# A hybrid encoder trunk on one core: gating values in the buffers of squares, the row of norms ahead in ScalarE's queue, first weights by single contraction steps

## The chip, the core and the metric

The kernel runs on one core of a Trainium2 chip. The core has TensorE (PE in the profile; its weight loads, which overlap, are PEld), VectorE (DVE), ScalarE (ACT), GpSimd (POOL) and SyncE (SP), which here only issues DMAs. TensorE reads its operands from on-chip memory and writes its sums into PSUM, of which this kernel uses eight banks of 128 x 512 floats. The metric is the device time in microseconds (us); lower is better.

## The reference

One layer over x (2048 x 1024, float32). The rows of x are normed by their root mean square, and one projection of 1024 x 2816 gives eleven slots of 256 columns, which four mixers share:

```python
h = rmsnorm(x, norm_g); proj = h @ w_in
a_u, a_v, a_g, b_q, b_k, b_v, b_g, c_in, c_g, d_q, d_g = split(proj, 11)
y_a = a_u * spatial_gating(layernorm(a_v)) * silu(a_g)       # 128x128 mixing per chunk and head
y_b = neighbourhood_attention(b_q, b_k, b_v) * silu(b_g)     # 8x16 windows on a 32x64 grid, 4 heads
y_c = fourier_mixing(c_in) * silu(c_g)                       # real part of a 2-D DFT, linear map
y_d = memory_attention(d_q, mem) * silu(d_g)                 # 256 memory tokens, 4 heads
out = x + concat(y_a, y_b, y_c, y_d) @ w_out
```

Queries and keys of both attentions are normed per head of 64.

## The kernel before

**Precision.** Nearly every product is made of three: each operand is split into a rounded part (hi) and the rest (lo), and hi x hi, hi x lo and lo x hi are summed in PSUM. The split of x is an ACTIVATE on ScalarE with the norm's weights as scale (L137) and a DVE instruction for lo (L138); the split of weights is a cast on ScalarE (L217, L229) and a subtraction on POOL or DVE (L219, L231).

**Order.** TensorE's instructions stand in the order in which the program writes them. A driver keeps a modelled time t, runs tasks that are due (attention, transposes, the Fourier part) and fills in products of projections otherwise; a task says by `yield d` after how many modelled us it wants to go on. The order of all other engines, SP's loads among them, is planned when the program is built: of what is ready in a planned run the instruction with the lowest number goes first, and `hp(n)` lowers the number by n. Each engine then works its list strictly in order. Buffers and banks are given out in the planned order as well; a tile waits until the buffer's former user is done.

**Stages.** The rows are worked in halves of 1024 (h = 0, 1). The first projection does two slots side by side, c_in with its accumulators in the four banks "acc", and d_q (`alt`) in the banks "sc" and "mi" (two each); it goes through the eight contraction steps k of 128 rows one by one. In each step come four groups, each of three products of c_in with 512 columns and six of d_q with 256. `get_w` loads weights for two steps at once (128 x 2 x 256, 256 KB) into one of five buffers "raw" and splits them. Eighteen transposes of a constant go ahead of the first product. `stats` squares the rows of x on ScalarE (L291) and gives rstd. `do_dq` norms d_q per head (`head_norm`: squares into one of two buffers "sq", L376; sums, L378) and transposes it in four parts. `bcast` transposes rstd into a bank "mi", copies it on ScalarE into a row (L302), writes it out and reads it back on all partitions. `mem_kv` projects the memory tokens and norms the keys, using "sq" too (L505, L376).

`pair_vv` then projects a_v and b_v together, in two passes u of 96 products of 512 columns, with four accumulators that hold 256 columns of each. `evac_vv` frees them: for each of four row tiles ScalarE or DVE scales the gating values a_v into half of a tile `va` (L456, L454), ScalarE writes hi of b_v (L459), DVE lo (L460), and SP stores b_v to V (L463). `va` (two per pass) and the tiles of b_v (four) all come from the five buffers "nat". `do_a` norms the gating values and TensorE reads them in `s_mix`, with 4.0 and 1.5 modelled us between. Then come a_u, the pair b_q and b_k, the gates and the same for the second half; d_0's attention, the Fourier part and the neighbourhood attention run beside them as tasks, the attentions through `pipeline`, which runs scores two units ahead of transposes. The output projection ends the program.

## Time and profile before

| | us |
|---|---|
| time of the kernel, median of 3 runs | 872.89 (871.86 to 875.16) |
| the profiled execution, its own time | 873.72 |
| its span in the profile | 872.0 |
| PE busy | 852.2 (98%), 4448 instructions |
| DVE busy | 501.8 (58%) |
| ACT busy | 407.4 (47%) |
| POOL busy | 327.3 (38%) |
| DMA | 177.88 MB, mean 204 GB/s |

Times in the profile count from the start of the span. Matmuls are pipelined, and the end of one is modelled, so busy shares of PE say where it stood still rather than how well it worked. "PEclk" is the clock that was granted to TensorE, as a share of full speed; it has two levels, 2.4 and 1.2 GHz (1.00 and 0.50). A bracket behind an instruction is the idle time of its engine before it, and what ended that.

### The profile page before, as it was taken

How to read it: one execution, taken by the hardware profiler on the slowest of the kernel's cores; microseconds unless marked ns; L12 is line 12 of the kernel's file. 1: busy time of each engine (PE TensorE's matmuls, PEld its weight loads, DVE VectorE, ACT ScalarE, POOL GpSimd, SP SyncE). 2: the span in 40 equal slices, each digit the busy share in tenths (PEclk: the TensorE clock that was granted, in tenths of full speed). 3: DMA queues.
4: the chain of work that ended last, by engine and by line, in shares of the span. 5: the costliest groups of instructions: out<-in, count | busy, mean ns of one | idle time of the engine just before them, and what ended most of it. 6: DMA issues, size and time to landing. Idle time of an engine off the chain costs nothing.

```text
span 872.0 us, 13653 instructions
## 1 busy us (share of the span) xinstructions
PE 852.2 (98%) x4448; PEld 713.5 (82%) x4448; DVE 501.8 (58%) x1064; ACT 407.4 (47%) x930; POOL 327.3 (38%) x368
## 2 busy tenths in 40 slices
PE   8999899999999999999999999999998999999998
PEld 7987688888788878887789888888877888888886
DVE  5355565587532557765454876676798778741111
ACT  5674353466742543544324644666767445521110
POOL 1136331154332122552232723434557333235550
PEclk9999999999999999999999999999999999999999
DMA  8957643346762562469759797864598986556661
GB/s 268 332 197 226 194 137 103 119 117 179 230 186 98 191 218 85 135 169 272 221 180 320 248 306 250 260 215 145 171 307 247 343 258 219 173 167 198 190 215 72
DMA packets 147463, 177.88 MB, mean 204 GB/s; under 512 B 29232, under 2 KB 105152, under 8 KB 147392
## 3 DMA queue, kind: packets, MB, share of 16 engines
q1 hardware_dynamic: 145104, 170.33, 62.4%
q0 software_dynamic: 1728, 6.29, 2.4%
q8 instruction: 35, 0.57, 0.3%
q10 hardware_dynamic: 560, 0.40, 0.1%
q14 instruction: 36, 0.29, 0.1%
HBM read 132.92 MB, written 44.05 MB: 203 GB/s over the span
## 4 chain that ended last, share of the span: by engine, by line
PE 72%; DMA 12%; DVE 6%; ACT 4%; issue 3%; POOL 2%; SPq 0%; ACTq 0%; DVEq 0%; POOLq 0%
PE acc L147 55%; PE w L147 8%; PE w L151 4%; PE sc L147 3%; PE mi L147 2%; DMA G<-st 2%; DMA nat<-in_mem 1%; DMA QD<-st 1%; DMA raw<-in_xT 1%; DVE PT L535 1%; POOL hss L125 1%; DMA kk<-KB 1%; DMA nat<-O 1%; DMA qq<-QB 1%; ACT P L918 1%
## 5 line engine op out<-in xcount | busy, mean ns | idle before, releaser
L147 PE MATMUL acc<-hilo 128*128 128x512 f32 (+1 forms) x2880 | 709.9, 389 | 6.5 <-DVE nat L460 3.2
L147 PEld LDWEIGHTS acc<-hilo 128*128 128x128 f32 x2880 | 510.1, 189 | 98.4 <-issue 4.0
L219 POOL TENSOR_TENSOR hilo<-raw,hilo 128x512 fp32r<-128x512 f32 x52 | 68.5, 1318 | 173.1 <-ACT hilo L217 145.4
L231 POOL TENSOR_TENSOR hilo<-raw,hilo 128x512 fp32r<-128x512 f32 x32 | 43.3, 1353 | 115.4 <-ACT hilo L229 94.8
L983 POOL TENSOR_TENSOR nat<-nat 128x256 f32<-128x256 f32 x48 | 37.3, 778 | 94.6 <-DMA nat<-O 73.4
L229 ACT CAST hilo<-raw 128x512 fp32r<-128x512 f32 x64 | 39.7, 621 | 65.5 <-PE acc L147 56.3
L535 DVE TENSOR_TENSOR PT<-w,PT 128x512 fp32r<-128x512 f32 (+2 forms) x96 | 61.2, 638 | 7.2 <-ACT PT L534 7.0
L918 ACT ACTIVATE P<-P,smx 128x288 f32<-128x288 f32 (+1 forms) x64 | 39.9, 623 | 54.2 <-DVE smx L916 54.2
L1027 DVE TENSOR_TENSOR st<-acc,st 128x512 f32<-128x512 f32 (+1 forms) x33 | 21.6, 672 | 71.8 <-PE acc L147 70.4
L534 ACT CAST PT<-w 128x512 fp32r<-128x512 f32 (+2 forms) x96 | 52.1, 543 | 21.7 <-PE w L151 21.3
L989 ACT CAST hilo<-nat 128x256 fp32r<-128x256 f32 x64 | 25.7, 406 | 75.7 <-PE acc L147 66.2
L151 PE MATMUL w<-ident,P 128*128 128x128 f32 (+1 forms) x352 | 54.2, 273 | 1.3 <-DVE tmp L954 1.1
L151 PEld LDWEIGHTS w<-ident,P 128*128 128x128 f32 (+1 forms) x352 | 43.1, 136 | 14.6 <-DVE tmp L954 1.5
L217 ACT CAST hilo<-raw 128x512 fp32r<-128x512 f32 x51 | 31.3, 618 | 46.7 <-PE acc L147 34.1
L916 DVE CUSTOM_DVE_ANT_0 P<-w,bt 128x288 f32<-128x288 f32 (+1 forms) x64 | 35.6, 556 | 13.5 <-PE w L147 6.8
L125 POOL TENSOR_TENSOR hss<-hss,mhalf 128x8 f32<-128x8 f32 x25 | 42.7, 1713 | 1.5
L958 POOL TENSOR_TENSOR ob<-tmp 64x128 f32<-64x128 f32 x64 | 30.1, 490 | 27.5 <-DVE tmp L954 26.4
L231 DVE TENSOR_TENSOR hilo<-raw,hilo 128x512 fp32r<-128x512 f32 x32 | 22.0, 689 | 31.6 <-ACT hilo L229 31.5
L607 ACT ACTIVATE P<-w,smx 128x256 f32<-128x256 f32 x64 | 29.8, 470 | 21.0 <-DVE smx L603 20.4
L921 DVE TENSOR_SCALAR P<-P,smx 128x288 f32<-128x288 f32 (+1 forms) x64 | 35.8, 560 | 1.8
L138 DVE SCALAR_TENSOR_TENSOR hilo<-raw,gcol,hilo 128x512 fp32r<-128x512 f32 x32 | 25.9, 818 | 18.9 <-ACT hilo L137 18.5
L345 DVE TENSOR_TENSOR st<-acc,rbc 128x512 f32<-128x512 f32 x32 | 21.9, 684 | 25.6 <-PE acc L147 22.2
(170 smaller groups left out, 1061.0 us busy)
## 6 DMA issues: line engine op xcount, KB each, us to landing
raw<-in_w_in SPq DMA_DIRECT2D x119, 256.0 KB, 3.4
raw<-in_xT SPq DMA_DIRECT2D x32, 256.0 KB, 3.8
nat<-in_x SPq DMA_DIRECT2D x32, 256.0 KB, 5.3
G<-st SPq DMA_DIRECT2D x32, 256.0 KB, 3.2
nat<-G SPq DMA_DIRECT2D x64, 128.0 KB, 2.5
st<-in_x SPq DMA_DIRECT2D x32, 256.0 KB, 4.9
out_y<-st SPq DMA_DIRECT2D x31, 256.0 KB, 2.9
tab<-in_dft_s POOLq DMA_DIRECT2D x12, 512.0 KB, 5.1
```

What stands on the lines that cost most here:

```text
L125: nc.gpsimd.tensor_tensor(out=out, in0=out, in1=self.mhalf[:, :n], op=ALU.pow)
L147: self.nc.tensor.matmul(out=out, lhsT=lhsT, rhs=rhs, start=start, stop=stop, **k)
L151: self.nc.tensor.transpose(out=out, in_=in_, identity=self.ident)
L219: eng.tensor_tensor(out=w[1], in0=raw, in1=w[0].bitcast(F32), op=ALU.subtract)
L229: nc.scalar.copy(out=w[0], in_=raw)
L231: eng.tensor_tensor(out=w[1], in0=raw, in1=w[0].bitcast(F32), op=ALU.subtract)
L534: self.nc.scalar.copy(out=hi, in_=src)
L535: (eng or self.nc.vector).tensor_tensor(out=lo, in0=src, in1=hi.bitcast(F32), op=ALU.subtract)
L916: nc.vector.tensor_tensor_reduce(out=P[:, :n], in0=sc[:, :n], in1=bt[:, :n], op0=ALU.add, op1=ALU.min, scale=-1.0, scalar=3e38, accum_out= ...
L918: nc.scalar.activation(out=P[:, :n], in_=P[:, :n], func=AF.Exp, bias=sm[:, 1:2], scale=-1.0, accum_out=sm[:, 2:3])
L921: nc.vector.tensor_scalar(out=P[:, :n], in0=P[:, :n], scalar1=sm[:, 3:4], scalar2=None, op0=ALU.mult)
L983: mul.tensor_tensor(out=g, in0=o, in1=g, op=ALU.mult)
```

## The change

Four edits. Gating values: `va` is taken from the two buffers "sq" instead of the five buffers "nat". Row of norms: the ACTIVATE of L302 gets `hp(9000)`; before, it had its plain number. First weights: for the first weights of c_in and of d_q only step 0 (128 x 256, 128 KB) is loaded ahead, both from ScalarE's queue (before: c_in's whole pair from ScalarE's queue, d_q's from SP's), with `hp(80000)`; hi of c_in comes from DVE as before, hi of d_q from ScalarE, lo from POOL and DVE. The second step's half is loaded by SP, copied and subtracted by POOL (c_in) or DVE (d_q) in `rest()`, which is called when the slot comes to step 1. The first weights of all later slots have `hp(8000)` instead of `hp(15000)`. In `pipeline` 1.5 modelled us more stand behind each of the first two scores.

```diff
 def get_w(self, name, k, c0, alt):
-        with self.hp(8000 if k or alt else 15000 if self.wseen else 80000):
+        with self.hp(8000 if k or self.wseen > 1 else 80000):
             raw = self.raw.tile([128, 2, 256], F32, name="raw")
-            begin = not self.wseen and not alt
-            self.wseen = True
-            (nc.scalar if begin else nc.sync).dma_start(out=raw, in_=self.ins[name][...].rearrange("(t p) c -> p t c", t=2))
+            begin = k == 0 and self.wseen < 2
+            self.wseen += 1
+            src = self.ins[name][k * 128:(k + 2) * 128, c0:c0 + 256].rearrange("(t p) c -> p t c", t=2)
+            if begin:
+                nc.scalar.dma_start(out=raw[:, 0], in_=src[:, 0])
+            else:
+                nc.sync.dma_start(out=raw, in_=src)
...
+            eng = nc.vector if alt else nc.gpsimd
             if begin:
-                nc.vector.tensor_copy(out=w[0], in_=raw)
+                (nc.scalar.copy if alt else nc.vector.tensor_copy)(out=w[0][:, 0], in_=raw[:, 0])
+                eng.tensor_tensor(out=w[1][:, 0], in0=raw[:, 0], in1=w[0][:, 0].bitcast(F32), op=ALU.subtract)
             else:
                 nc.scalar.copy(out=w[0], in_=raw)
-            eng = nc.vector if alt else nc.gpsimd
-            eng.tensor_tensor(out=w[1], in0=raw, in1=w[0].bitcast(F32), op=ALU.subtract)
+                eng.tensor_tensor(out=w[1], in0=raw, in1=w[0].bitcast(F32), op=ALU.subtract)
+        if begin:
+            def rest():
+                with self.hp(8000):
+                    nc.sync.dma_start(out=raw[:, 1], in_=src[:, 1])
+                    eng.tensor_copy(out=w[0][:, 1], in_=raw[:, 1])
+                    eng.tensor_tensor(out=w[1][:, 1], in0=raw[:, 1], in1=w[0][:, 1].bitcast(F32), op=ALU.subtract)
+            self.rest[alt] = rest
 def slot(self, h, c0, natural, ps, kstep):
+            elif k0 == 1 and alt in self.rest:
+                self.rest.pop(alt)()
 def bcast(self, h):
-        nc.scalar.activation(out=row, in_=ps, func=AF.Copy, scale=0.5)
+        with self.hp(9000):
+            nc.scalar.activation(out=row, in_=ps, func=AF.Copy, scale=0.5)
 def evac_vv(self, h, u, ps):
-                    va = self.nat.tile([128, 512], F32, name="nat")
+                    va = self.sqp.tile([128, 512], F32, name="sq")
 def pipeline(self, items, d):
-                yield d[0]
+                yield d[0] + (1.5 if n < A else 0)
```

## Rows read from the trace of the kernel before

**Rows 1.** The page, part 1: busy us, share of the span, instructions.
```profile
PE 852.2 (98%) x4448; PEld 713.5 (82%) x4448; DVE 501.8 (58%) x1064; ACT 407.4 (47%) x930; POOL 327.3 (38%) x368
```
**Rows 2.** TensorE's waits by releaser: us in total, times, longest us.
```profile
PE acc L147 <- DVE nat L460: 3.2, 3, 1.6
PE w L147 <- DVE PT L535: 2.6, 4, 1.9
PE mi L151 <- ACT sa_o L302: 1.9, 1, 1.9
```
**Rows 3.** Timeline of the start: start us, us, engine, line, operation, tiles, count, [idle before].
```profile
5.29 0.72 ACT L137 ACTIVATE hilo<-raw,gcol 128x512 fp32r<-128x512 f32 x1 [0.47 <-DMA raw<-in_xT]
5.86 0.43 DVE L215 CAST hilo<-raw 128x512 fp32r<-128x512 f32 x1 [0.25 <-DMA raw<-in_w_in]
6.37 1.70 POOL L219 TENSOR_TENSOR hilo<-raw,hilo 128x512 fp32r<-128x512 f32 x1 [5.07 <-DVE hilo L215]
6.43 0.70 PE L147 MATMUL acc<-hilo 128*128 128x512 f32 x2 [0.98 <-DVE hilo L215]
6.59 0.62 ACT L217 CAST PT<-raw 128x512 fp32r<-128x512 f32 x1 [0.57 <-DMA raw<-in_w_in]
7.24 1.38 DVE L219 TENSOR_TENSOR PT<-raw,PT 128x512 fp32r<-128x512 f32 x1 [0.29 <-ACT PT L217]
8.12 0.50 PE L147 MATMUL acc<-hilo 128*128 128x512 f32 x1 [0.99 <-POOL hilo L219]
9.80 1.48 PE L147 MATMUL acc<-hilo 128*128 128x512 f32 x3
```
**Rows 4.** Window from 5 to 6 us: busy by engine, PEclk, DMA share, GB/s.
```profile
5.00:6.00 1.00, 0.45 (x3) 0.05 (x1) 0.75 (x2) 0.70 (x1) 0.00 (x0) 1.00 1.09 393
```
**Rows 5.** Windows around TensorE's stalls: busy by engine, PEclk, DMA share, GB/s.
```profile
8.90:12.13 3.23, 3.23 (x13) 2.94 (x13) 2.08 (x5) 1.01 (x3) 0.00 (x0) 0.50 0.80 268
97.89:101.10 3.21, 3.21 (x8) 2.54 (x9) 2.54 (x7) 0.62 (x1) 1.59 (x3) 0.52 0.64 163
73.00:75.30 2.30, 0.44 (x3) 0.07 (x2) 0.85 (x2) 1.99 (x6) 0.90 (x3) 1.00 0.86 281
```
**Rows 6.** Timeline around the row of norms, 73 to 76 us.
```profile
73.31 0.63 ACT L495 ACTIVATE nat<-nat 128x512 f32<-128x512 f32 x1 [1.93 <-DMA nat<-in_mem]
74.92 0.26 ACT L302 ACTIVATE sa_o<-mi 8x128 f32<-8x128 f32 x1
75.24 0.66 PE L151 MATMUL mi<-ident,nat 128*128 128x128 f32 x4 [1.86 <-ACT sa_o L302]
```
**Rows 7.** Timeline of the first pass's evacuation, 86 to 98 us.
```profile
86.12 0.59 ACT L534 CAST st<-mi 128x512 fp32r<-128x512 f32 x1 [5.70 <-DMA QD<-st]
89.03 0.76 DVE L508 TENSOR_TENSOR vm<-sq,vm 128x256 fp32r<-128x256 f32 x2 [1.59 <-ACT vm L507]
93.33 0.45 DVE L454 TENSOR_SCALAR nat<-acc,rstd 128x256 f32<-128x256 f32 x1
94.70 0.48 ACT L459 ACTIVATE nat<-acc,rstd 128x256 fp32r<-128x256 f32 x1 [2.15 <-DMA V<-nat]
95.21 0.48 DVE L460 SCALAR_TENSOR_TENSOR nat<-acc,rstd,nat 128x256 fp32r<-128x256 f32 x1 [1.43 <-ACT nat L459]
95.74 0.96 PE L147 MATMUL acc<-hilo 128*128 128x512 f32 x3 [1.64 <-DVE nat L460]
97.89 4.43 PE L147 MATMUL acc<-hilo 128*128 128x512 f32 x12 [1.19 <-DVE nat L460]
```
**Rows 8.** Timeline around the end of the second pass, 116 to 126 us.
```profile
116.36 7.10 PE L147 MATMUL acc<-hilo 128*128 128x512 f32 x30
117.23 0.61 ACT L217 CAST hilo<-raw 128x512 fp32r<-128x512 f32 x1
124.99 0.48 ACT L459 ACTIVATE nat<-acc,rstd 128x256 fp32r<-128x256 f32 x1 [1.66 <-DVE nat L454]
```
**Rows 9.** The chain that ended last, its last piece: start us, us, what.
```profile
769.27 98.62 PE acc L147 x435
```

## Prediction before the result

> **What bounds the kernel now.** The busy times come first: TensorE works 852.2 of 872.0 us [rows 1]. No other engine can set the time over a long stretch; what a change can win is TensorE's idle time, some 20 us, and stretches in which its clock is low. The waits of TensorE by releaser show what the idle time is made of [rows 2]: 3.2 us for the vector step L460 that frees an accumulator, 2.6 us in four waits for PT (L535), 1.9 us for the row of norms (L302). The timeline then gives each its place: the row's wait is one, before the transposes at 75.24 [rows 6]; 1.64 and 1.19 us of L460's are at 95.74 and 97.89 [rows 7]; and the start has two more, 0.98 us up to 6.43 and 0.99 us up to 8.12 [rows 3]. Last the windows: the granted clock is 0.50 of full, the lower of its two levels, from 8.90 to 12.13, behind the two waits of the start, and 0.52 from 97.89 to 101.10, behind the two of L460 [rows 5]. It was 1.00 through the 1.86 us of the row's wait and in the 3 us after it [rows 5, 6]. So the two double stalls are paid twice.
>
> **First weights by single contraction steps.** Now c_in's first product waits for the copy L215: weights land at 5.86, the copy takes 0.43 us, and TensorE starts 0.14 us after it [rows 3]. DVE was idle for 0.25 us before that copy, so free from 5.61. 393 GB/s came in at that time [rows 4], so 128 KB less are 0.33 us, and the half lands at about 5.5. Copy of half the columns, half of 0.43: 5.61 to 5.83; first product at 5.97, 0.46 us earlier. The third product needs the subtraction on POOL: 1.70 us for the whole, an estimated 0.85 for the half; it begins 0.08 us after the copy as now, ends at 6.76, and the product starts at 6.81 instead of 8.12. d_q's half comes behind c_in's on ScalarE's queue at about 5.9. ScalarE is in L137 from 5.29 to 6.01; its copy of half the 0.62 us of L217 ends at 6.35. DVE has to scale x's second tile first and then subtracts, half of 1.38 at most [rows 3]: about 7.2 to 7.5. The next group of c_in then starts at about 8.0 where it started at 9.80: 1.8 us.
>
> TensorE's idle time from 5.45 to 8.1 shrinks from 1.97 to about 0.9 us. For the clock the rows bound both sides: after 1.97 us in two pieces it fell, after one of 1.86 us it didn't [rows 3, 5, 6]. 0.9 us is nearer to the second, so I take no fall; that saves the part of the low stretch behind 9.80, (12.13 - 9.80) x 0.5 = 1.2 us. The start brings 1.8 + 1.2 = 3.0 us; if the clock falls as before and the copies come in a worse order, 1.2.
>
> What is added: two loads on SP, two copies and two subtractions for the second steps. They are needed when step 1 begins, three groups after 8.0: each has three products of 0.236 us [rows 8] and six of half the columns, counted at half of that, 1.42 us in all, so at about 12.3. Their data can be there by 7.5. On DVE copy and subtraction cost at most half of 0.43 + 1.38 [rows 3]; the copy on POOL isn't in this trace, I bound it by 0 and by POOL's 1.70 and take half of that. All is ready by about 9.5, so it costs nothing; without that cover it would be some 2 us. The two raw buffers come free at about the same time as now (8.1 and 8.6, the ends of the two L219).
>
> The trace gives 393 GB/s for all queues together [rows 4]; it can't show who waits for whom. The Trainium skill, "DMA: Bandwidth & Descriptors", section "Issuing engines are not separate DMA queues", says that loads issued by different engines share the same sixteen DMA engines and interleave, so that another issuing engine saves only issue time. By that rule d_q's half, now on ScalarE's queue, delays x's second tile by up to 0.33 us, an estimate, and the start brings 2.7 us, not 3.0.
>
> **The row of norms.** It runs on ScalarE at 74.92, queued behind L495, which sat 1.93 us until 73.31 for a load of mem. The row's input is a transposition that stands 12 products ahead of the stall in TensorE's list; at 7.10 / 30 = 0.236 us each [rows 8] it was done 2.8 us before the stall began at 73.38, so at 70.6, before L495's wait began at 71.38. It holds one of two banks, and the transposes at 75.24 wait 1.86 us for it [rows 6]. Ahead in the queue it costs its 0.26 us of ScalarE before L495, which waits for a load anyway. The stall goes whole: 1.86 us. The bank that is late next is the one of the transposes before the row, which only the transposes after these ask for. Bounds 0 to 1.86. The broadcast load behind the row comes earlier too, and its consumer is not on TensorE's path.
>
> **Gating values in the buffers of squares.** Six tiles of the buffers "nat" per half pass become four, and with the memory tokens' one that is five, the number there is. L459 then no longer waits 2.15 us for the store of V at 94.70 and 1.07 us later on. DVE ends L454 at 93.78 [rows 7]; 0.48 us of L459 and 0.48 of L460 behind it give 94.7 for the third tile, where TensorE had run dry at 94.10 (95.74 - 1.64), and the fourth follows 0.5 us later. Of 2.83 us I leave 0.3 for ScalarE's and DVE's own pace: 2.5 gained, 0 to 2.83 the bounds. The new wait: the gating values need a "sq" buffer, whose users before them end with L508 at 89.8 [rows 7], 0.3 us behind the present first write; the memory keys' squares may queue behind the gating values, but their result goes to products that stand behind both reads in TensorE's list. With the stall goes the low clock: 3.21 x 0.48 = 1.5 us.
>
> **Pauses and priorities.** 1.5 us more between the first two units of a pipeline moves when TensorE's list takes attention, not how much. At the end 435 plain products follow the last unit [rows 9], more than the 384 that need it, so a delay of 3 us is covered. It shifts where attention meets the other work: the remaining waits may shrink or grow, and I bound this by the largest of them, 2.6 us to either side [rows 2], and take 0. First weights of later slots drop from 15000 to 8000 in priority; the cast at 117.23 comes before the evacuations at any rate, since it is ready earlier [rows 8]: 0.
>
> **Sum.** 3.0 + 1.86 + 2.5 + 1.5 = 8.9 us. Not all arrives together: at 86.12 ScalarE ends 5.70 us of waiting for a store of QD [rows 7], and loads and stores come forward by less than TensorE does. TensorE would be 4.9 us early there; I let this chain come 3.1 us early, and 1.8 us turn into a wait for the evacuations behind it. 7.1 us remain: 873.72 - 7.1 = 866.6 for the profiled execution, which was 0.8 above the median; so 865.8.
>
> **Rivals.**
> 1. The start and the row give less: d_q's copy is queued ahead of x's scaling on ScalarE, the clock falls again, or the row is planned behind L495 still, so that it doesn't do what it says. For: the order is planned ahead with other arrival times. Against: the present order has x first. Loses 1.8 of the start and 0.9 of the row: 868.5.
> 2. The evacuation stays late: ScalarE's wait for QD's store doesn't move, or a gating tile waits for a "sq" buffer held by the memory's square. For: 5.70 us idle on that store. The stalls at 95.74 stay with their low clock, and only some 3 us of the lead survive: 869.9.
> 3. Slower: the lowered priority. Behind the last evacuation, which ends at 125.47, the cast of a_u's first weights would come 8 us later than at 117.23 [rows 8]. TensorE asks for them 27 products into the run at 116.36, at 122.7; after 0.62 of cast and about 1.3 of subtraction on POOL they would be there at 127.4: 4.7 us, and 1.5 more when the clock falls. Three slots stand so behind a pair. It decides from two slots on, 2 x 6.2 = 12.4 against the 7.1: 872.9 + 5.3 = 878.2; with all three 18.6 - 7.1 = 11.5 more, 884.4. Against: the cast's buffer is free before the evacuation can begin.
> 4. The shifted attention meets the rest badly: 2.6 back, 868.4, or as much less.
>
> **Chances.** Forecast 0.58 (862.5 to 868.4); rival 1 0.18; rival 2 0.12; rival 3 0.05; rival 4 on the bad side 0.07. About 0.5% (4.4 us) is what a measurement can tell from none, so faster means below 868.5: 0.56 + 0.08 + 0.02 + 0.03 = 0.69. Slower by over 0.5%: 0.05. Same: 0.26. The range reaches down to the whole 8.9 us and 2.6 less of remaining waits, 861.5, and up past rival 2, 871.5.
>
> **What would show it.** The profile after should have TensorE's third product near 6.8 and no stretch of clock 0.5 before 13 us; L302 within a microsecond of 70 and no wait before the second transposes; no L459 waiting for V's store, and clock 1.00 near 95. A wait for L215 or L217 beyond 6.5, a wait for the evacuation of 2 us or more, or a new wait for POOL's L219 after a pair would make it wrong.

## The result and the profile after

The changed kernel is slower: 879.54 us, median of 8 runs (876.10 to 881.37), against 874.10 for 8 runs of the kernel before beside them; the ratio is 1.0069, 95% interval 1.0053 to 1.0085. The forecast was 865.8 us, its range ended at 871.5, and slower by over 0.5% had a chance of 0.05. The profiled execution took 878.81 us with a span of 876.9; before it was 873.72 and 872.0. Single executions of the kernel before lie between 869.51 and 878.33 us, so below a span places a loss, and only a ratio with its interval says whether there is one.

Lines have moved by 2 at the weights and by 14 from `evac_cin` on: L316 is the row (L302 before), L318 and L320 its store and its broadcast read (L304, L306), L324 the multiply of c_in by the norms (L310), L433 QD's store (L419), L473 and L474 the halves of b_v (L459, L460), L509 the squares of mem (L495), L522 the memory values' lo (L508), L688 the normalisation of the gating values (L674).

Busy times on the page, part 1, against [rows 1]; then TensorE's waits by releaser (us in total, times, longest us), against [rows 2]:

```profile
PE 854.7 (97%) x4448; PEld 714.3 (81%) x4448; DVE 502.2 (57%) x1066; ACT 406.0 (46%) x930; POOL 333.3 (38%) x370
```
```profile
PE w L147 <- DVE PT L549: 6.3, 6, 2.5
PE acc L147 <- DVE sa L683: 3.6, 1, 3.6
PE acc L147 <- DVE nat L474: 2.4, 2, 2.0
```

Work has grown by next to nothing. The wait for the row is gone and the two for L460 have changed their shape: 3.6 us now end with L683, an instruction of the gating norm, and 2.0 with L474. The waits for PT went from 2.6 to 6.3. The first product of a memory score is a good mark between the two places, since TensorE has no wait between 105 us and it in either kernel:

```profile
123.30 0.63 PE L147 MATMUL w<-km,dq 128*128 128x256 f32 x4
```
```profile
125.71 0.63 PE L147 MATMUL w<-km,dq 128*128 128x256 f32 x4
```

The first line is of before, the second of after, both from the timeline (start us, us, what). So 2.4 us of the 4.9 are lost up to the mark, and 2.5 behind it (748.7 from mark to end before, 751.2 after).

**The start** [rows 3]. SP's list and the timeline of the first microseconds, after:

```profile
1.64 0.43 SPq L227 DMA_DIRECT2D raw<-in_w_in  x1
2.12 0.43 SPq L195 DMA_DIRECT2D raw<-in_xT  x1
2.59 0.43 SPq L227 DMA_DIRECT2D raw<-in_w_in  x1
...
5.84 0.72 ACT L137 ACTIVATE hilo<-raw,gcol 128x512 fp32r<-128x512 f32 x1 [0.76 <-DMA raw<-in_xT]
...
6.04 0.29 DVE L219 CAST hilo<-raw 128x256 fp32r<-128x256 f32 x1 [5.14 <-DMA raw<-in_w_in]
6.25 1.88 DVE L138 SCALAR_TENSOR_TENSOR hilo<-raw,gcol,hilo 128x512 fp32r<-128x512 f32 x2
8.05 0.61 DVE L220 TENSOR_TENSOR PT<-raw,PT 128x256 fp32r<-128x256 f32 x1
...
6.48 1.65 PE L147 MATMUL acc<-hilo 128*128 128x512 f32 x3 [1.18 <-DVE hilo L219]
```

The second halves (L227) go out at 1.64 and 2.59, among x's loads. In this execution the first half lands at 6.04, where the whole pair landed at 5.86, and x's second tile at 5.84 instead of 5.29. The granted clock is 0.55 from 8.90 to 12.13 (before 0.50), and contraction step 1 of c_in begins at 15.04 (before 15.15).

These two executions are no fair pair, since the start scatters from one execution to the next. Of the kernels profiled for this document nine have the new start (after and experiments 1, 3, 4, 6, 9, 12, 13, 16) and nine the old one (before and experiments 2, 5, 7, 10, 14, 15, 17, 18). Lowest to highest, and the middle one, in us:

| start of | new start | old start |
|---|---|---|
| the copy of c_in's first weights | 5.05 to 6.04, 5.58 | 5.86 to 6.34, 6.09 |
| the second group of c_in | 8.56 to 9.95, 9.47 | 9.53 to 10.48, 10.21 |
| contraction step 1 of c_in | 12.80 to 15.04, 14.22 | 15.15 to 16.44, 15.48 |
| the last sum of x's squares | 55.85 to 57.13, 56.13 | 53.80 to 55.43, 54.53 |
| the transposition of rstd | 70.62 to 72.33, 70.90 | 70.33 to 71.63, 70.65 |

So the new start brings some 1.3 us at step 1; the two executions above set the latest of one nine against the earliest of the other. Near 70 us nothing of it is left (in the two executions 71.27 against 70.33, which is 0.9 of the 2.4 us up to the mark). The squares end later, the copies of c_in stand among them in ScalarE's list, and TensorE waits for these copies, 0.39 us in the kernel after and up to 2.2 us (experiment 16). Of the nine only experiment 1 has no such wait; with the old start none has a wait between 20 and 70 us.

```profile
57.21 3.71 PE L147 MATMUL acc<-hilo 128*128 128x512 f32 x15 [0.39 <-ACT cin L338]
```

**The row of norms** [rows 6]. ScalarE, TensorE and SP, after:

```profile
71.54 0.56 ACT L548 CAST st<-mi 128x512 fp32r<-128x512 f32 x1
...
76.47 0.63 ACT L509 ACTIVATE nat<-nat 128x512 f32<-128x512 f32 x1 [3.84 <-DMA nat<-in_mem]
...
77.09 0.25 ACT L316 ACTIVATE sa_o<-mi 8x128 f32<-8x128 f32 x1
...
74.16 0.60 PE L151 MATMUL mi<-ident,nat 128*128 128x128 f32 x4
...
77.37 0.34 SPq L318 DMA_DIRECT2D rs<-sa_o  x1
...
78.32 0.56 SPq L590 DMA_DIRECT2D dq<-QD  x1
79.28 1.46 SPq L433 DMA_DIRECT2D QD<-st  x2
80.83 0.58 SPq L320 DMA_DIRECT2D rbc<-rs  x1
```

and SP's list before:

```profile
77.57 0.34 SPq L306 DMA_DIRECT2D rbc<-rs  x1
78.43 0.56 SPq L576 DMA_DIRECT2D dq<-QD  x1
79.08 1.22 SPq L419 DMA_DIRECT2D QD<-st  x2
```

The row still stands behind L509 and its wait for mem, and that wait is longer. The transposes start at 74.16 without a wait all the same, because ScalarE had read the other bank at 71.54, ahead of L509. And SP's list has changed: between the row's store and the broadcast read stand a load of dq and two stores of QD. The read goes out at 80.83; in the kernel before it went at 77.57, ahead of those.

**The first evacuation** [rows 7]:

```profile
82.60 4.75 POOL L310 TENSOR_TENSOR cin<-cin,rbc 128x1024 f32<-128x1024 f32 x2 [3.56 <-DMA rbc<-rs]
```
```profile
86.95 4.93 POOL L324 TENSOR_TENSOR cin<-cin,rbc 128x1024 f32<-128x1024 f32 x2 [6.42 <-DMA P<-in_dft_d]
...
87.70 4.46 DVE L522 TENSOR_TENSOR vm<-sq,vm 128x256 fp32r<-128x256 f32 x2 [1.30 <-ACT vm L521]
...
92.26 0.47 ACT L470 ACTIVATE sq<-acc,rstd 128x256 f32<-128x256 f32 x1 [1.97 <-DVE vm L522]
...
93.92 2.54 PE L147 MATMUL acc<-hilo 128*128 128x512 f32 x9 [2.05 <-DVE nat L474]
...
97.05 1.58 DVE L688 TENSOR_SCALAR sq<-sq,sa 128x256 f32<-128x256 f32 x2
98.56 0.68 DVE L527 COPY PT<-nat 128x1024 f32<-128x1024 f32 x1
...
99.50 0.46 DVE L474 SCALAR_TENSOR_TENSOR nat<-acc,rstd,nat 128x256 fp32r<-128x256 f32 x1
...
100.10 2.48 PE L147 MATMUL acc<-hilo 128*128 128x512 f32 x6 [3.64 <-DVE sa L683]
```

The first line is of before, the others of after. GpSimd's multiply, which waits for the broadcast, ran from 82.60 to 87.35 before. (In the kernel after its row names a load of P, which the multiply doesn't read; in experiment 9 the row of the multiply in the same place names rbc.) Now it runs from 86.95 to 91.88, and in that time VectorE's two subtractions L522 take 4.46 us; the same two took 0.76 in [rows 7]. They read the buffers of squares, which the gating values now want, so the first gating write waits until 92.26 (89.16 before) and TensorE runs dry at 91.87. Then the fourth accumulator: its last reader L474 stands in VectorE's list behind the normalisation of the first two tiles and a copy for the memory's keys, and TensorE waits 3.64 us more. The two instructions of this normalisation are stretched as well: 1.58 us beside a split of weights on GpSimd (96.86 to 98.17), where the kernel before takes 0.73 for two. From 100.10 to 104.00 the granted clock is 0.56; it was 0.52 behind the stalls of before [rows 5].

VectorE beside GpSimd is what the trace shows: the splits end at 92.16, 0.28 us after the multiplies. The Trainium skill, "SBUF — State Buffer", section "Who interferes with whom", says that the two engines share a pair of SBUF ports as an exclusive lock: an instruction of VectorE with two inputs in SBUF, and one of GpSimd that reads SBUF, run one behind the other. The trace agrees: the two instructions of some 0.38 us take 1.92 and 2.62 us beside two multiplies of some 2.5 us, and each ends 0.28 us after a multiply (89.62 after 89.34, 92.16 after 91.88).

**Behind the mark**, near 650 us, the timeline after, and a window (start:end, length, busy by engine, clock, DMA share, GB/s):

```profile
646.94 1.59 DVE L935 TENSOR_SCALAR P<-P,smx 128x384 f32<-128x384 f32 x1
...
647.05 1.26 POOL L135 TENSOR_TENSOR hilo<-raw,hilo 128x512 fp32r<-128x512 f32 x1
...
649.56 1.40 PE L147 MATMUL w<-PT,vt 128*128 128x512 f32 x5 [2.50 <-DVE PT L549]
```
```profile
646.00:656.00 10.00, 7.50 (x31) 6.04 (x30) 8.93 (x18) 4.78 (x12) 5.88 (x9) 0.83 0.93 295
```

An instruction that takes 0.41 us elsewhere takes 1.59 beside GpSimd, the split behind it is late, and TensorE stands 2.50 us and then runs at a lowered clock (0.58 from 649.56 to 653.00).

### The profile page after: what moved, and what is told of

Same layout as the page of the kernel before. It is cut to its first block, busy times and chain, and to the rows that moved or that the text cites. A ratio compares the mean times of both kernels' runs of the same rounds, so it can differ in the third digit from the quotient of the medians.

```text
span 876.9 us, 13657 instructions
## 1 busy us (share of the span) xinstructions
PE 854.7 (97%) x4448; PEld 714.3 (81%) x4448; DVE 502.2 (57%) x1066; ACT 406.0 (46%) x930; POOL 333.3 (38%) x370
## 4 chain that ended last, share of the span: by engine, by line
PE 78%; DVE 7%; DMA 7%; ACT 4%; POOL 3%; issue 2%; SPq 0%; ACTq 0%; DVEq 0%; POOLq 0%
PE acc L147 59%; PE w L147 8%; PE w L151 4%; PE sc L147 3%; PE mi L147 2%; DMA G<-st 1%; DMA nat<-in_mem 1%; POOL hss L125 1%; DMA raw<-in_xT 1%; DMA bt<-in_bias 1%; DVE hilo L1004 1%; DMA nat<-O 1%; DVE PT L549 1%; DMA raw<-in_w_in 1%; DVE vm L522 1%
## 5 line engine op out<-in xcount | busy, mean ns | idle before, releaser
L147 PEld LDWEIGHTS w<-PT,vt 96*128 96x128 f32 (+1 forms) x160 | 27.5, 190 | 13.5 <-DVE PT L549 8.5
L147 PE MATMUL w<-PT,vt 96*128 96x256 f32 (+3 forms) x160 | 32.3, 333 | 6.1 <-DVE PT L549 6.1
```

The costliest lines, as they stand in the source:

```text
L147: self.nc.tensor.matmul(out=out, lhsT=lhsT, rhs=rhs, start=start, stop=stop, **k)
```

## Experiments

"First score" is the mark above (before 123.30, after 125.71), read from one execution of each kernel. The scatter of the start goes into it (rstd from 70.33 to 71.63 with one and the same start), so differences of about 1 us say little. All ratios are to the kernel before on the same chip.

**1. No multiply.** The kernel after without GpSimd's multiply of c_in (which leaves c_in unscaled).

```diff
-            for cj in range(2):
-                nc.gpsimd.tensor_tensor(out=self.cin[cj][:, 0:HS], ..., in1=bc, op=ALU.mult)
+            pass
```

> The changed kernel without the two multiplications of c_in by the broadcast norms on POOL (L324; the first half of c_in stays unscaled, so this part of the computation is left out). Theory A (collision): the row of norms came later, so these multiplications (4.93 us on POOL from 86.95) fell on the split of the memory values on DVE (L522, 4.46 us for two instead of 0.76), which holds the buffers of squares and DVE's queue; without them L522 takes under 1 us for two, the first gating value is written by 89.5 instead of 92.26, TensorE's wait before the third accumulator falls from 2.05 us to under 0.5, the one before the fourth from 3.64 to under 2, and the time is 3 to 5 us lower. Theory B (buffers): the gating values wait for buffers of squares whoever is on POOL; L522 stays short or long without effect and both waits stay above 1.5 us each.

Measured: 870.45 us in a single execution, first score 119.95. VectorE's splits, and TensorE's only wait between 60 and 105 us:

```profile
86.87 0.76 DVE L521 TENSOR_TENSOR vm<-sq,vm 128x256 fp32r<-128x256 f32 x2 [1.69 <-ACT vm L520]
...
96.01 2.96 PE L147 MATMUL acc<-hilo 128*128 128x512 f32 x12 [2.93 <-DVE sa L682]
```

The splits take 0.76 us again, the start of the evacuation is no longer late, and the clock stays at 1.00 (12 products in 2.96 us). The fourth accumulator's wait stays: it is a loss of its own.

**2. No weights' edit.** The kernel after with `get_w` as before.

```diff
-            elif k0 == 1 and alt in self.rest:
-                self.rest.pop(alt)()
...
-            if begin:
-                nc.scalar.dma_start(out=raw[:, 0], in_=src[:, 0])
+            (nc.scalar if begin else nc.sync).dma_start(out=raw, in_=src)
```

> The changed kernel with the edit of the first weights undone (one load per pair, old queues and priorities; row, gating values and pause stay changed). Theory A with the first weights as the start of the chain: the squares of x end near 53.9 again instead of 56.5, the row is written near 75 instead of 77.09, the multiplications on POOL start near 82.6, L522's two take under 1 us, and the two waits at 92 to 100 us (5.7 us) fall below 2.5; time 871 to 874. Rival: the start's loads have nothing to do with it; the row still comes after 77 and the waits stay, time 877 to 880.

Measured: ratio 1.0037 (1.0018 to 1.0057), broadcast read at 77.61, multiply from 82.51, splits 0.76 us, first score 123.61. So it is the edit of the first weights that sets the collision off. All other kernels bear this out: where the broadcast read goes out from SP's queue, it goes at 79.94 to 81.40 in the ten with this edit, and at 77.00 to 78.56 in the eight without it. Which part of the edit moves it, the two loads, their copies or the lower priority of later first weights, no run separates. What is left of the change still loses: one wait of 3.40 us stays near 98 us, and the time is above the 871 to 874 us that I gave. The row, with its new priority, comes at 74.97, still behind the wait for mem, and the transposes wait 1.59 us for it.

**3. Row on VectorE.** The kernel after with the row made by VectorE, so that it can't stand behind L509.

```diff
-            nc.scalar.activation(out=row, in_=ps, func=AF.Copy, scale=0.5)
+            nc.vector.tensor_scalar(out=row, in0=ps, scalar1=0.5, scalar2=None, op0=ALU.mult)
```

> The changed kernel with the row of norms written by DVE (tensor_scalar by 0.5) instead of ScalarE, where it sat behind L509's wait for a load until 77.09. Theory A: DVE writes it by about 73, the broadcast arrives by about 79, the multiplications on POOL run before 85, L522's two take under 1 us, and TensorE's two waits at 92 to 100 us (5.7 us) fall below 2.5 together; time 872 to 875. Theory B (the buffers of squares, or DVE's own order): the row is early, but the waits stay within 1 us of 5.7; time 877 to 880.

Measured: ratio 1.0070 (1.0048 to 1.0091). The row is ready at 72.37 and stored at 73.16, but the broadcast read goes out at 80.12, behind dq and QD's stores; multiply from 86.00, splits 4.23 us. My theory that the late row makes the late broadcast fell: it is SP's list.

**4. No pause.** The kernel after without the 1.5 modelled us in `pipeline`.

```diff
-                yield d[0] + (1.5 if n < A else 0)
+                yield d[0]
```

> The changed kernel without the 1.5 modelled us behind the first two scores of a pipeline. Theory: the pause moved the neighbourhood attention against the end of the second half's gates and cost TensorE's waits for PT from 550 to 660 us (4.2 us, before 0.2) and the low clock behind them; undone, the waits of 550 to 660 fall to about 1.8 as before, the waits at 92 to 100 stay at 5.7, and the time is 2 to 3 us below the changed kernel's 879.5. Rival: those waits come from the later arrival of everything after 100 us; they stay, and the time is 879 to 880.

Measured: ratio 1.0073 (1.0047 to 1.0099), splits 5.16 us, first score 127.60. Near 90 us the pause isn't the cause. Behind the mark it decides where the waits fall, not how much is lost: without it the waits for PT between 550 and 660 us go from 4.2 to 0.7 us, as expected, and the stall near 650 with them, but another of 1.83 us comes at 673 with a lowered clock behind it, and from mark to end it takes 750.8 us (after 751.2).

**5 and 6. One edit alone**, on the kernel before: the gating values', and the first weights' (the diffs of the change).

```diff
-                    va = self.nat.tile([128, 512], F32, name="nat")
+                    va = self.sqp.tile([128, 512], F32, name="sq")
```

> The kernel before with one edit: the gating values' tile comes from the buffers of squares. Theory A (the wait for V's stores is only exchanged for a wait in VectorE's queue): the broadcast and the multiply stand where they stood before (multiply from about 82.6 us), the two splits of the memory values take 0.76 us together, no wait for V's stores, but the fourth accumulator's evacuation comes behind the normalisation of the first two tiles and TensorE waits about 3.4 us for it before 100 us; first score on the memory's keys at about 123.5 us, 872 to 874 us, ratio 1.000 to 1.003. Rival B (the prediction's own step): the 2.83 us of waits go and with them 1.5 us of low clock: 868 to 870 us.

> The kernel before with the edit of the first weights alone. Theory A (this edit moves the broadcast of norms behind dq's load and QD's stores in SyncE's list): broadcast issued near 80.8 us, multiply on GpSimd from near 87 us, the two splits of memory values stretched to 4 us or more together, the gating tile's evacuation 3 us later than before; 875 to 878 us, ratio 1.002 to 1.006. Rival B (the stretch costs only where the gating values want the buffers of squares): the splits are stretched, yet the waits near 90 to 100 us sum to no more than before's 2.8 us; 872 to 873.5 us.

Measured: 1.0038 (1.0020 to 1.0056) for the gating edit, 1.0030 (1.0011 to 1.0048) for the weights; together 1.0068, the change's 1.0069. TensorE with the gating edit alone:

```profile
97.55 4.49 PE L147 MATMUL acc<-hilo 128*128 128x512 f32 x12 [3.16 <-DVE sa L669]
```

The 2.83 us of V's store [rows 7] have turned into 3.16 us of VectorE's queue, with a lowered clock behind them as before (0.59 from 97.55 to 101.50). So the gain isn't had. The loss of 0.38% isn't in this trace, though: the first score, 123.02, is 0.28 us earlier than before, and the profiled execution, 873.57 us, is the shortest of ten with a median of 876.38. Where the longer executions lose their time no trace here shows. With the weights' edit alone:

```profile
86.82 0.76 DVE L521 TENSOR_TENSOR vm<-sq,vm 128x256 fp32r<-128x256 f32 x2
...
92.14 1.73 POOL L242 TENSOR_TENSOR hilo<-raw,hilo 128x512 fp32r<-128x512 f32 x1
...
93.92 1.42 PE L147 MATMUL acc<-hilo 128*128 128x512 f32 x5 [2.70 <-POOL hilo L242]
...
97.91 0.47 ACT L472 ACTIVATE nat<-acc,rstd 128x256 fp32r<-128x256 f32 x1 [7.16 <-DMA V<-nat]
```

Here I expected stretched splits, and they aren't: they ran at 86.82, and the multiply began at 87.44. It costs in another way: TensorE waits 2.70 us for weights whose lo stands behind the multiply in GpSimd's own list, and V's store holds ScalarE as before. Here the profiled execution (876.67) is like the median (876.65), and the trace accounts for most of the loss: the first score, 125.30, is 2.0 us late. The transposes near 75 us, without the row's edit, start at 73.51 and don't wait:

```profile
73.51 0.60 PE L151 MATMUL mi<-ident,nat 128*128 128x128 f32 x4
```

The late multiply is the common cause, the stretch only one of its prices.

**7. One reciprocal root for both gating tiles**, with the gating edit alone, so that no normalisation can stand ahead of the fourth accumulator.

```diff
-            for v in vs:
-                sm = self.small.tile([128, 24], F32, name="sa")
+            sm = self.small.tile([128, 36], F32, name="sa", bufs=2)
+            for i, v in enumerate(vs):
...
-                self.rsqrt(sm[:, 16:18], mv[:, :, 1], 1.0, 2)
+            self.rsqrt(sm[:, 32:36], mv[:, :, 1], 1.0, 4)
```

> The kernel before with the gating edit, and with one reciprocal root for the two gating tiles instead of one each, so that no normalisation can be queued before the fourth accumulator's evacuation. Theory A: the wait for the fourth accumulator falls from about 3.4 us to under 1 us, the clock stays at its high level between 95 and 101 us, first score on the memory's keys at 119.5 to 120.5 us (before 123.3); 868 to 870 us, ratio 0.995 to 0.998. Rival B (the accumulator waits for something else, such as ScalarE's casts of weights): the wait stays over 2 us and the time is 872 us or more.

Measured: ratio 1.0018 (1.0001 to 1.0035), wait 2.28 us, first score 122.50. The rival's numbers hold: a split of weights (1.39 us beside GpSimd's) and the copy were still ahead. This run shows another thing. TensorE's wait at 667 us and the window behind it:

```profile
667.16 1.09 PE L147 MATMUL w<-PT,vt 128*128 128x512 f32 x5 [1.86 <-DVE PT L535]
```
```profile
668.00:672.00 4.00, 4.00 (x16) 3.38 (x15) 2.48 (x7) 1.94 (x5) 2.13 (x3) 0.57 0.92 277
```

and the kernel before at the same place:

```profile
667.60 1.08 PE L147 MATMUL w<-PT,vt 128*128 128x512 f32 x5 [1.87 <-DVE PT L535]
```
```profile
668.00:672.00 4.00, 4.00 (x23) 3.43 (x22) 3.13 (x10) 3.02 (x8) 1.96 (x3) 1.00 0.91 299
```

The same wait, once with the clock at 0.57 behind it (16 products in 4 us) and once at 1.00 (23 products).

**8. Halves held back.** The kernel after; the second halves' loads wait until x's second tile is split.

```diff
+                    nc.vector.tensor_copy(out=raw[:, 1, 0:1], in_=self.X[(0, 0)][1][1][:, 0:1].bitcast(F32))
                     nc.sync.dma_start(out=raw[:, 1], in_=src[:, 1])
```

> The kernel after, with the second halves of the first two weight loads issued only once the second tile of x has been split (a one-column copy of that tile is written into their buffer first). Theory A (the start gained nothing since the halves' loads share the memory bandwidth with x): x's second tile is split by ScalarE near 5.3 us instead of 5.84, the first product comes near 6.0 to 6.4 instead of 6.48, and the second contraction step starts 0.3 to 1 us before 15.04. Rival B (the low clock decides, not the loads): the second step starts within 0.2 us of 15.04. A third way: the halves are late and TensorE waits for them at the second step.

Measured: 879.47 us in a single execution. The first product comes at 5.69, the clock from 5 to 13 us is 1.00 (0.79 before), and step 1 begins at 12.77: 2.4 us ahead of before, more than I had expected. That holding the halves back brings this isn't shown: experiment 16 begins step 1 at 12.80 without it, and experiment 11, with it, at 14.56. The lead is given back here:

```profile
55.48 0.96 PE L147 MATMUL acc<-hilo 128*128 128x512 f32 x3 [1.27 <-ACT cin L339]
...
57.70 5.29 PE L147 MATMUL acc<-hilo 128*128 128x512 f32 x15 [1.26 <-ACT cin L339]
```

The copies of c_in stand in ScalarE's list among the squares of x, which wait for loads; those come no sooner, TensorE waits 2.5 us, and the clock falls (0.56 from 57.70 to 61.00).

**9. Multiply on VectorE**, in the kernel after.

```diff
-                nc.gpsimd.tensor_tensor(out=self.cin[cj][:, 0:HS], ..., in1=bc, op=ALU.mult)
+                nc.vector.tensor_tensor(out=self.cin[cj][:, 0:HS], ..., in1=bc, op=ALU.mult)
```

> The kernel after, with the multiply of c_in by the norms' factors on VectorE instead of GpSimd: no work is left out and no edit undone. Theory A (the loss near 90 us is GpSimd's multiply beside VectorE's splits): the two splits of the memory values take 0.76 us together again, the evacuation of the gating tile starts 2 to 4 us earlier than in the kernel after (92.3 us), and the first score on the memory's keys comes at 120 to 123.5 us (after: 125.7); ratio 0.998 to 1.003. Rival B (VectorE then stands waiting for the broadcast, which lands near 86 us, and the splits come as late as before): first score at 125 us or later, ratio 1.005 or more.

Measured: ratio 1.0045 (1.0029 to 1.0062), first score 126.59. The splits take 0.75 us, but start at 90.62: the rival holds (but for its ratio, put at 1.005 or more), VectorE stands for the broadcast.

```profile
87.75 2.36 DVE L324 TENSOR_TENSOR cin<-cin,rbc 128x1024 f32<-128x1024 f32 x2 [6.66 <-DMA rbc<-rs]
```

**10 and 11. Every wait so far taken out at once**, without and with the first weights (halves held back): the gating edit, one root, row on VectorE, memory's values in another buffer, the row's store and broadcast from GpSimd's queue.

```diff
-            v = self.sqp.tile([128, 256], F32, name="sq")
+            v = self.att.tile([128, 256], F32, name="od", bufs=2)
...
-        nc.sync.dma_start(out=d, in_=row)
+        nc.gpsimd.dma_start(out=d, in_=row)
-        nc.sync.dma_start(out=bc, in_=d.rearrange(...))
+        nc.gpsimd.dma_start(out=bc, in_=d.rearrange(...))
```

> The kernel before with the gating edit, one reciprocal root for both gating tiles, the memory's values in another buffer than the squares', the row of norms made by VectorE, and the row's store and broadcast issued from GpSimd's queue. Theory A (each wait named so far is one of queue and buffer): no wait of the transposes at 75 us (before 1.9), multiply from 80 to 81 us, gating tile evacuated from 89 us, wait for the fourth accumulator under 2 us and no low clock between 95 and 101 us; first score on the memory's keys at 118 to 120.5 us (before 123.3), 867 to 870 us. Rival B (the end of the memory's products sets it all): 121 us or later and 871 us or more.

> As the kernel without the weights' edit before it in this call, with the first weights by single contraction steps and their second halves' loads held until the second tile of x is split. Theory A (the start's gain of 2.4 us, seen with held-back halves, is real, and was lost in the late broadcast): the second contraction step starts at 12.8 us (before 15.15), first score on the memory's keys 1.5 to 2.5 us before that of the kernel without the edit; 865 to 868 us, ratio 0.992 to 0.996. Rival B (the squares of x end later, at 56 us, and TensorE waits for the norms): the 2.4 us are given back before 75 us.

Measured: 1.0009 (0.9988 to 1.0031) and 1.0038 (1.0015 to 1.0060); first scores 123.98 and 126.67. Both miss. The broadcast, issued by GpSimd at 78.60 and 81.83, let the multiply begin at 84.81 and 88.34, later than before's 82.60. In 11 it met the splits again (1.93 us for the first); in 10 it had ended at 89.59, and the first split, 1.03 us from 90.09, met the split of weights that stands behind it on GpSimd. In 11 step 1 begins at 14.56, not at 12.8 as I had expected, and TensorE waits 2.2 us for c_in's copies before 60 us, as in experiment 8.

**12. Lower halves of the gated outputs on GpSimd**, in the kernel after: a test of the stretch near 650 us.

```diff
-            (nc.gpsimd if q > 4 else nc.vector).tensor_tensor(out=y[:, 1], ..., op=ALU.subtract)
+            nc.gpsimd.tensor_tensor(out=y[:, 1], ..., op=ALU.subtract)
```

> The kernel after, with the output stage's lower halves (the split of gated outputs) on GpSimd in all eight groups, not the last three alone. Theory A (the wait of 2.5 us at 647 us and the low clock behind it come from VectorE instructions stretched beside GpSimd's; the split of the gated outputs took 2.38 us for two of 0.41 to 0.5): that wait and the low clock near 650 us go, and the stretch from the first score on the memory's keys to the end falls from 751.2 to 748 to 749.5 us. Rival B (GpSimd becomes the late one, or the stretch moves to the next instruction of VectorE): 751 us or more.

Measured: ratio 1.0141 (1.0110 to 1.0171); from mark to end 761.1 us. The wait at 649 us falls to 0.52 and the clock there is 1.00, as in the first theory, but the rival holds: with more work on GpSimd waits of 3.0, 2.8 and 2.2 us appear between 660 and 780. That the stretch of VectorE causes the loss near 650 isn't shown by this.

**13. Multiply later**, in the kernel after: held back until the memory's keys are split.

```diff
+        nc.vector.scalar_tensor_tensor(out=bc[:, 0:1], in0=self.km[1][:, 3, 255:256].bitcast(F32), scalar=0.0,
+                                       in1=bc[:, 0:1], op0=ALU.mult, op1=ALU.add)
         for cj in range(2):
             nc.gpsimd.tensor_tensor(out=self.cin[cj][:, 0:HS], ..., in1=bc, op=ALU.mult)
```

> The kernel after, with GpSimd's multiply of c_in put behind the splits of the memory's keys (near 110 us) and all else as it is: no instruction of the change is undone and none left out (a one-column operation on VectorE that changes no value holds it back). Theory A (the multiply beside VectorE's splits is what the change loses near 90 us): the two splits of the memory values take 0.76 us together, the gating tile's evacuation starts near 89 us (after: 92.3), first score on the memory's keys at 119.5 to 121.5 us (after 125.7, without the multiply 119.95); 869 to 873 us, ratio 0.996 to 1.001. Rival B (the loss only moves, since the multiply now stretches VectorE's work at 110 us): first score at 124 us or later.

Measured: the splits at 86.99 in 0.76 us, evacuation from 87.99 (after 92.26), first score 121.65: 4.1 us of the kernel after's way to the mark come back with all its work done. The multiply runs from 118.59 to 123.36. The first score is just outside what I gave, and the ratio, 1.0027 (1.0010 to 1.0043), above it: 751.4 us from mark to end, as in the kernel after.

**14. Attention values first.** The gating edit alone, and in `evac_vv` the block of b_v ahead of that of a_v; the fourth accumulator then goes ScalarE, VectorE and not VectorE, ScalarE, VectorE.

```diff
-                if j % 2:
-                    nc.vector.tensor_scalar(out=o, in0=ps[j][:, 0:256], scalar1=r, scalar2=None, op0=ALU.mult)
-                else:
-                    nc.scalar.activation(out=o, in_=ps[j][:, 0:256], func=AF.Copy, scale=r)
                 v = self.nat.tile([128, 4, 2, 64], F32R, name="nat")
...
+                if j % 2:
+                    nc.vector.tensor_scalar(out=o, in0=ps[j][:, 0:256], scalar1=r, scalar2=None, op0=ALU.mult)
+                else:
+                    nc.scalar.activation(out=o, in_=ps[j][:, 0:256], func=AF.Copy, scale=r)
```

> The kernel before with the gating edit, and with the attention values of each tile evacuated ahead of its gating values (two blocks of lines exchanged), so that the fourth accumulator needs one hand-over between ScalarE and VectorE less. Theory A: the wait for the fourth accumulator (3.2 us with the gating edit alone) falls under 1.5 us and the low clock behind it goes; first score on the memory's keys near 120 us (123.0 with the gating edit alone); 868 to 870.5 us, ratio 0.995 to 0.999. Rival B (splits of weights on VectorE, stretched beside GpSimd's, hold the fourth accumulator as before): wait over 2 us, 122 us or later.

Measured: ratio 0.9984 (0.9970 to 0.9998), 871.83 us, first score 118.54.

```profile
86.89 10.68 PE L147 MATMUL acc<-hilo 128*128 128x512 f32 x45
...
93.57 0.48 DVE L456 SCALAR_TENSOR_TENSOR nat<-acc,rstd,nat 128x256 fp32r<-128x256 f32 x1
...
94.36 1.59 DVE L674 TENSOR_SCALAR sq<-sq,sa 128x256 f32<-128x256 f32 x2
```

TensorE goes through all 45 products without a stall. VectorE reads the fourth accumulator at 93.57, ahead of the normalisation at 94.36. This is the prediction's gating step, had at last: 4.8 us up to the mark. The span of this execution is 4.1 us under before's, the ratio stands for 1.4 us; single executions scatter by more than the difference, and it isn't settled.

**15 and 16. Both repairs**, on the gating edit alone and on the whole change: multiply later, attention values first (the diffs of 13 and 14).

> As the kernel with gating edit and attention values first, with the multiply of c_in put behind the splits of the memory's keys as well. Theory A: it gives no more near 90 us, since there the multiply ends at 86.7 us before the splits begin; first score on the memory's keys within 0.5 us of that kernel's, the same time within 1 us. Rival B (the multiply at 82 to 87 us holds VectorE's bias and transposition work, 2.2 us instead of 0.3): 1 to 2 us less.

> The kernel after with both repairs: the multiply put later, and the attention values evacuated first. Theory A: the gain that the gating step was to bring is had once both new waits are gone: first score on the memory's keys at 118 to 120 us, 867 to 870 us, ratio 0.993 to 0.998. Rival B (what the queue gains near 90 us comes back as waits and low clock near 650 us, as in five of the kernels so far, whose stretch from that score to the end was 750 to 751 instead of 748.6 to 749.6 us): 870 to 872 us.

Measured: 0.9998 (0.9980 to 1.0017), first score 120.13; and 0.9980 (0.9964 to 0.9997), first score 118.72. The first shows no gain from a later multiply where it wasn't late; its mark is 1.6 us behind experiment 14's, but 1.05 of that stands already at the transposition of rstd (71.53 against 70.48). The whole change with two repairs is faster than the kernel before, by less than 0.5%; from mark to end it takes 751.5 us, so the second theory has its share.

**17 and 18. What carries it.** Attention values first on the kernel before, without the gating edit; and experiment 14 with the row on VectorE (diffs of 14 and 3).

> The kernel before with the attention values evacuated ahead of the gating values, and the gating tile left where it was. Theory A (gating tile in the buffers of squares and the new order are both needed): the tile still shares its buffers with V's stores, waits of 2 us or more stay between 93 and 98 us, first score on the memory's keys at 122 us or later, ratio 0.998 to 1.003. Rival B (the order alone does it): no wait over 1 us there, first score at 119 us, ratio 0.994 to 0.998.

> The kernel before with the gating edit, the attention values first, and the row of norms made by VectorE. Theory A (the row's wait is worth what the transposes wait for it): the 1.5 us before 75 us fall to about 0.5, first score on the memory's keys at 117.5 to 118.5 us, time 0.5 to 1.5 us under that of the kernel without the row's edit (871.8). Rival B (TensorE's lead of 1 us is taken back by the wait for the memory's products or the start of the evacuation at 88 to 89 us): first score at 118.5 us or later, no difference.

Measured: 1.0023 (1.0005 to 1.0041), first score 121.71. Waits of 1.10 and 1.01 us stay at 95.76 and 97.74, less than I had expected, and the clock is 1.00, but the mark and the ratio of experiment 14 aren't reached: both edits are needed. And 0.9965 (0.9950 to 0.9980), 870.89 us: the lowest ratio of all, with an interval that overlaps those of experiments 14 and 16. It is not had in the way expected, since its first score is at 119.10, the transposes still wait 0.78 us, and TensorE waits 0.68 us for the fourth accumulator:

```profile
95.13 3.00 PE L147 MATMUL acc<-hilo 128*128 128x512 f32 x12 [0.68 <-DVE sq L460]
```

## Why the prediction was wrong

**The start: 3.0 us predicted, some 1.3 came, and none of it was kept.** The landing was about right: the copy begins at 5.58 in the middle one of nine executions, where I had 5.61. The steps that failed stand behind it. "The next group of c_in then starts at about 8.0 where it started at 9.80: 1.8 us": it starts at 9.47, against 10.21 with the old start, so 0.7. VectorE scales both of x's first tiles between the copy and d_q's subtraction (6.25 to 8.13 in the kernel after; before, the first of them stood ahead of the copy, at 4.86), and the subtraction, put at "about 7.2 to 7.5", ends at 8.66. TensorE waited 1.18 and 0.47 us where I had 0.9, and the clock, "I take no fall", was 0.55 from 8.90 to 12.13 in that execution. The last step I didn't write down at all: that a lead at 15 us lasts. By 70 us it is gone, since the copies of c_in come later with the squares of x.

**The row: 1.86 us predicted; the wait is gone, by another cause.** The row did not move ahead (77.09, behind L509): the case I had under rival 1. What freed the transposes was the other bank, read earlier, and that came with the edit of the weights: with it and the row's old priority they don't wait (experiment 6), with the new priority and the old weights they wait 1.59 us (experiment 2). The sentence that cost most stands at the end of this step: "The broadcast load behind the row comes earlier too, and its consumer is not on TensorE's path." It came 3.3 us later, and its consumer is GpSimd's multiply, beside which VectorE's splits stretch and behind which a weights' split stands.

**Gating: 2.5 us and 1.5 of clock predicted; by itself 0.28 us came up to the mark, and the time is 0.38% longer.** The wait for V's store went, as worked out. What I named next, the buffers of squares, was one new wait; I placed the end of L508 at 89.8 as now, and with the late multiply it is 92.16. The other I didn't see: the fourth accumulator "follows 0.5 us later", but the gating norm no longer waits, so VectorE has it in its list ahead of that accumulator's reader: 3.16 us alone, 3.64 in the change. (By my own numbers 2.2 us was the most, not 2.5: the third accumulator comes free at 94.7, TensorE is dry from 94.10.) I had followed the tile that was waited for, and not the work that its coming free lets in.

**Pauses and priorities: 0 predicted.** Near 90 us this holds (experiment 4). Behind the mark the change loses 2.5 us, within the 2.6 that I had left to either side but on top of everything else; without the pause the waits stand elsewhere and the loss stays.

**The rivals.** Rival 2 names the wait for a buffer of squares, held by the memory's square; it was held by the memory's values. Rival 3, slower by a lowered priority, is not what happened: no wait for a_u's weights appears. No rival had a transfer that moves back in SP's list, though the change puts two loads into that list; that is why the chance of slower was 0.05.

**What stays open.** Two losses. The gating edit alone costs 0.38%, and the one execution in which it was profiled doesn't contain that loss. And the loss behind the mark: from the mark to the end the kernels took between 748.6 and 752.1 us (experiment 12 aside), one execution each. The edit of the weights sorts them best: 748.7 to 750.1 in the nine without it, 750.8 to 752.1 in eight of the ten with it, but 749.6 where it stands alone (experiment 6) and 748.6 without the multiply (experiment 1), so it isn't the edit as such. The stretched instruction beside GpSimd near 650 us is seen in the trace; that it makes the difference is argued, and experiments 4 and 12, which both remove the stall there and win nothing, don't bear it out.

## What to carry to other kernels

When an edit adds or moves a transfer, write out the whole list of the queue around it and follow each transfer behind it to its consumer, then to what that consumer shares a buffer or an engine with: here one broadcast read 3.3 us late, off TensorE's path, set GpSimd against VectorE. When a wait is taken away, ask which instructions become ready with it, and whether they now stand ahead of the one that frees the accumulator; the order of two blocks of lines (experiment 14) did what a buffer alone didn't. Run each edit alone before trusting a sum: 1.0038 and 1.0030 add up to about the change's 1.0069, where the sum had a gain of 0.8%. And price a stage from several executions: one pair of traces put the gain of the new start at 0.1 us, nine on each side at 1.3.

## What the runs showed of the hardware that was not expected

- Two subtractions of 128 x 256 with both inputs in on-chip memory took 0.76 us on VectorE, and 4.46 beside GpSimd's multiplies of 128 x 1024 (4.93 us for the two, 4.80 in experiment 5): VectorE pays nearly all.
- The size of a wait doesn't tell what the clock does: 1.87 us at 667 us left it at 1.00 in the kernel before, 1.86 us at the same place put it to 0.57 in experiment 7, and 2.93 us in experiment 1 left it at 1.00. My rule from [rows 3, 5, 6], that one wait of 1.9 us is free and two are not, was drawn from too few.
- From the issue of the broadcast read to its consumer's start it took 4.4 us in experiment 18 (77.49 to 81.85), 5.0 before (77.57 to 82.60), 6.1 after (80.83 to 86.95) and 7.5 in experiment 6 (79.94 to 87.44), the same 512 KB on the receiving side each time.
- The same first loads reached their consumer at 5.05 to 6.04 us in nine executions with the new start, and contraction step 1 began at 12.80 to 15.04.
